# A diffusion step on one core: another share for the long convolution, a smaller prompt pool, and weight halves kept in DRAM

## The chip, the core and the metric

The kernel runs on one core of a Trainium2 chip. Its engines are TensorE (PE, matmuls; PEld loads its stationary operand), VectorE (DVE), ScalarE (ACT), GpSimd (POOL) and SyncE (SP). They run side by side, each through its own instruction queue in order, and wait for each other by semaphores; 16 DMA engines move data between DRAM and the core's memory (SBUF). The metric is the device time of one execution in microseconds, the median of several. Matmul results land in PSUM.

## What is computed

One trunk layer of a hybrid diffusion model, for 2048 latent tokens (`x_sample`) and 256 prompt tokens (`x_prompt`) of width 1024, all in float32. Cut to what matters here:

```python
def trunk_layer(x, cond, attend, ...):
    shift1, scale1, gate1, shift2, scale2, gate2 = adaln(cond, w_mod, b_mod)
    h = rms_norm(x, norm1_g) * (1.0 + scale1) + shift1
    u = h @ w_in                       # 1024 -> 256 pool + 768 hyena + 512 q + 512 k + 512 v
    y_pool = pool_mixer(u_pool, ...)   # centred windows 2/4/8/16
    y_hy = hyena_mixer(u_hy, ...)      # width-3 convolution, then two gated long convolutions by FFT
    q = rms_norm(u_q, q_norm_g); k = rms_norm(u_k, k_norm_g)
    y_na = attend(q, k, v)             # latent: 2-D neighbourhood and cached keys; prompt: dense
    x = x + gate1 * (concatenate([y_pool, y_hy, y_na]) @ w_out)
    h = rms_norm(x, norm2_g) * (1.0 + scale2) + shift2
    return x + gate2 * (square(relu(h @ w_up)) @ w_down), k, v
```

The same weights serve both groups of tokens. The outputs are both groups' tokens and the prompt's keys and values.

## The kernel before

**Precision.** A float32 matmul is done as three matmuls of a shorter type (float32r): `split` (L106) makes of each operand a high half (a copy that rounds, on ScalarE or POOL, L112 or L114) and a low half (operand less high half, L115), and `mm3` (L125) adds high by high, high by low and low by high. Weights come in tiles of 128 x 1024 (512 KB): `wtile` (L118) loads one by SP's queue into `wraw` (three buffers) and splits it into `wh` and `wl` (pool `w`, three buffers each); VectorE makes every low half.

**Streams.** The program is written as three generators that `weave` (L172) interleaves: `dense` (L1173), `latent_mixers` (L1050) and `prompt_mixers` (L851). Each yields a cost after each piece of work; `weave` always goes on with the stream whose sum of costs, divided by its share (2200e3, 850e3 and 700e3), is the least, and a stream that has to wait for another's result yields None until then, its sum standing still. This sets the order of the program and the priority of each instruction; the latent stream gets a lead of 1000 in priority and the prompt stream one of 2500. When the program is built, a list scheduler puts each engine's instructions into their final order by these priorities and by when their inputs and buffers are ready on its own timeline. I call the shares and this scheduler the planner.

**Dense.** The 2304 tokens are five runs: four of 512 latent tokens and one of 256 prompt tokens. First, in the order 0, 1, 2, 4 (the prompt), 3, each run is normalised and multiplied with the eight tiles of `w_u` (pool and convolution columns, L1193 to L1197), with 24 matmuls of the run's length on each tile. Then, in the order 3, 4, 0, 1, 2, `proj_qkv` (L257) multiplies each run with the twelve tiles of `w_qkv`, in six jobs of two tiles (L281, L282). The tokens are the stationary operand here and 256 columns of weights move, so that a job of a 512-token run is 96 matmuls; the first of its two tiles has its last use 12 matmuls before the end (L293, L294). The high half of the second tile of a job is made by POOL. After the projections the stream waits for the prompt stream (L1225), then runs `head` (output projection, L1084) and `mlp` (L1117) for the prompt and for the four latent runs.

**Latent mixers.** `filters` (L454) make the convolution's filters and bring them and the input to frequencies, with DFT matrices that POOL's queue loads (`dft_load`, L370). Then `hyena` (L615) does a spectral pass of 16 steps (`spectrum`, L622, in pool `p2v`), eight steps back to time and forth again (`inverse` and `fwd1`, pool `p2w`), a second spectral pass (pool `p2x`) and a last way back (`p2y`). Then comes the attention (L1065 on), which by the stream's order waits for the convolution, the projections and the prompt.

**Prompt mixers.** After the prompt's projections are written into the program (L852): the prompt's filters (L712), then in one pool `phy` the prompt's long convolution (L749) and the pooling of all tokens (L804), interleaved, then the prompt's attention (L922). The prompt's convolution begins with `conv3` (L563) for six channel tiles. Pools of SBUF are stacked from both sides: the prompt's lie on the right, beside those of the projections, and the latent mixers' on the left. A pool that covers an address of a closed pool waits for the last use of the tile that lay there.

Of the kernel before, what the change touches and what calls it, by code (L numbers as in the profile page):

```python
# [10 lines left out]
F32 = mybir.dt.float32  # L11
F32R = mybir.dt.float32r
# [7 lines left out]
P = 128  # L20
# [35 lines left out]
def tile_hybrid_step(ctx: ExitStack, tc: tile.TileContext, a: dict):  # L56
    nc = tc.nc
# [60 lines left out]
    def wtile(name, i, k, hi_eng=None):  # L118

        shape = [P, k, 1024 // k]  # L120
        raw = wp.tile(shape, F32, tag="wraw", name="wraw", bufs=3)
        nc.sync.dma_start(out=raw, in_=a[name][i].rearrange("p (k c) -> p k c", k=k))
        return split(wp, raw, shape, "w", nc.vector, hi_eng=hi_eng)

    def mm3(out, lh, ll, rh, rl, start, stop, **kw):  # L125
        nc.tensor.matmul(out, lh, rh, start=start, stop=False, **kw)  # L126
        nc.tensor.matmul(out, lh, rl, start=False, stop=False, **kw)  # L127
        nc.tensor.matmul(out, ll, rh, start=False, stop=stop, **kw)  # L128
# [28 lines left out]
    def normed(pool, x, r, g, s, k, bufs, keep=False):  # L157

        n = x.shape[1]
        t = xp.tile([P, 512], F32, tag="raw", name="xn", bufs=3)[:, :n] if keep else x  # L160
        if k % 2:
            hi = pool.tile([P, 512], F32R, tag="hh", name="hh", bufs=bufs)[:, :n]
            lo = pool.tile([P, 512], F32R, tag="hl", name="hl", bufs=bufs)[:, :n]
            nc.vector.scalar_tensor_tensor(out=t, in0=x, scalar=g, in1=r, op0=ALU.mult, op1=ALU.mult)  # L164
            nc.scalar.activation(hi, t, AF.Identity, bias=s)
            nc.vector.scalar_tensor_tensor(out=lo, in0=t, scalar=s, in1=hi.bitcast(F32), op0=ALU.add, op1=ALU.subtract)  # L166
            return hi, lo
        nc.gpsimd.tensor_tensor(out=t, in0=x, in1=r, op=ALU.mult)
        nc.vector.tensor_scalar(out=t, in0=t, scalar1=g, scalar2=s, op0=ALU.mult, op1=ALU.add)  # L169
        return split(pool, t, [P, 512], "h", nc.gpsimd, n=n, bufs=bufs)  # L170

    def weave(*streams):  # L172

# [83 lines left out]
    def proj_qkv(qp, hT, T0, n):  # L257

        todo = []

        def rows(dst, r0, cs):
            return dst[r0:r0 + 2 * P, cs].rearrange("(e p) c -> p e c", p=P)

        def finish(comp, part, t, raw, r, out):

            heads = raw.rearrange("p (e h d) -> p (e h) d", e=2, h=4)
            nc.vector.tensor_tensor(out=heads, in0=heads, in1=r[:, t // 32:t // 32 + 8, None].to_broadcast([P, 8, DH]), op=ALU.mult)
            tr = aux_tile()
            for c in range(2):
                for e in range(2):  # L270
                    nc.tensor.transpose(tr[:, (2 * c + e) * P:(2 * c + e + 1) * P], raw[:, e * 256 + c * P:e * 256 + (c + 1) * P], ident)
            nc.scalar.activation(out[:, :, t:t + 256], tr.rearrange("p (c t) -> p c t", c=2), AF.Copy, scale=(qg8, pvs("kg"))[comp])
            if t + 256 < n:
                return
            for c in range(2):
                j = 2 * part + c
                nc.sync.dma_start(out=(qT, kT)[comp][j][:, T0:T0 + n], in_=out[:, c])
                if comp == 1 and T0 == NL:
                    nc.sync.dma_start(out=a["new_kT"][j * P:(j + 1) * P, :], in_=out[:, c])

        for comp, part in JOBS:  # L281
            W = [wtile("w_qkv", 4 * comp + 2 * part + kk, 4, (None, nc.gpsimd)[kk]) for kk in range(2)]  # L282
            cs = slice(part * 256, (part + 1) * 256)
            out = raws = None
            if comp < 2:
                out = qp.tile([P, 2, 512], F32, tag="qo", name="qo")[:, :, :n]
                ss = qp.tile([P, 16], F32, tag="ss", name="ss")[:, :n // 32]
                raws = []
            for t in range(0, n, 2 * P):
                pp = acc_tile()  # L290
                for e in range(2):
                    ts = slice(t + e * P, t + (e + 1) * P)
                    for k in range(KD):  # L293
                        mm3(pp[:, e * 256:(e + 1) * 256], hT[k][0][:, ts], hT[k][1][:, ts], W[k // 4][0][:, k % 4, :], W[k // 4][1][:, k % 4, :], k == 0, k == KD - 1, skip_group_check=True)  # L294
                    if e == 0 and todo:
                        finish(*todo.pop(0))
                    yield 2600
                v = qp.tile([P, 512], F32, tag="q", name="v", bufs=3)
                nc.scalar.activation(v, pp, AF.Copy)
                if comp < 2:  # L300
                    sq = xp.tile([P, 512], F32, tag="tmp", name="sq")
                    nc.scalar.activation(sq, v, AF.Square)
                    nc.vector.tensor_reduce(out=ss[:, t // 32:t // 32 + 8], in_=sq.rearrange("p (h d) -> p h d", d=DH), axis=AX.X, op=ALU.add)
                    raws.append((t, v))
                    continue
                v2 = v.rearrange("p (e c) -> p e c", e=2)
                if T0 < NL:
                    nc.sync.dma_start(out=rows(vd, T0 + t, cs), in_=v2)
                else:
                    nc.sync.dma_start(out=rows(vpd, 0, cs), in_=v2)  # L310
                    nc.sync.dma_start(out=rows(a["new_v"], 0, cs), in_=v2)
            if comp < 2:
                r = rstd(qp, ss, DH, [P, n // 32], "small")
                todo += [(comp, part, t, v, r, out) for t, v in raws]
        while todo:
            finish(*todo.pop(0))
# [244 lines left out]
                fs1d.append((yield from filter_latent(o)))  # L561

    def conv3(hy, j, t0, L):  # L563
        u = hy.tile([P, L], F32, tag="cu", name="cu", bufs=2)
        nc.sync.dma_start(out=u, in_=uT[2 + j][:, t0:t0 + L])
        y = hy.tile([P, L], F32, tag="cy", name="cy", bufs=2)
        nc.scalar.activation(y, u, AF.Identity, scale=pvs("cw1", j), bias=pvs("cb", j))
        nc.vector.scalar_tensor_tensor(out=y[:, 1:L], in0=u[:, 0:L - 1], scalar=pvs("cw0", j), in1=y[:, 1:L], op0=ALU.mult, op1=ALU.add)
        nc.vector.scalar_tensor_tensor(out=y[:, 0:L - 1], in0=u[:, 1:L], scalar=pvs("cw2", j), in1=y[:, 0:L - 1], op0=ALU.mult, op1=ALU.add)
        return y  # L570
# [479 lines left out]
    def latent_mixers():  # L1050
        with scope("aps", 1, space=PSUM) as aps:
# [8 lines left out]
            yield from wait_for("u")  # L1060
            yield from wait_for("ln")
            with scope("hy") as kp:
                yield from hyena(kp, psum)
            done.add("hyena")
        yield from wait_for("qkv", "prompt")  # L1065
        with scope("att") as at, scope("attps", 2, space=PSUM) as aps:
# [106 lines left out]
    def dense(ms):  # L1173
# [3 lines left out]
        with scope("ln", side="right") as lp:  # L1177
# [8 lines left out]
            for i, b in enumerate(UORD):  # L1186
# [4 lines left out]
                if i < 4:  # L1191
                    xs = norm1_load(lp, *run_of(UORD[i + 1])[:2])
                for step, ct in enumerate((6, 2, 0, 7, 3, 4, 1, 5)):  # L1193
                    wh, wl = wtile("w_u", ct, 8)
                    pp = acc_tile()[:, :n]
                    for k in range(KD):
                        mm3(pp, wh[:, k, :], wl[:, k, :], hT[k][0], hT[k][1], k == 0, k == KD - 1)  # L1197
# [273 lines left out]
```

## Time and profile before

| | |
|---|---|
| median of 3 runs | 3198.05 us (3195.04 to 3200.3) |
| the profiled execution | 3199.58 us |
| its span, first to last instruction | 3197.7 us |
| TensorE (PE) busy | 3044.0 us, 95% of the span |
| its weight loads (PEld) | 2512.5 us, 79% |
| VectorE (DVE) busy | 1939.3 us, 61% |
| ScalarE (ACT) busy | 1427.5 us, 45% |
| GpSimd (POOL) busy | 958.1 us, 30% |
| mean granted clock of TensorE | 0.970 |
| moved by DMA | 494.26 MB, 154 GB/s of DRAM traffic over the span |

Times in the rows count from the first instruction. In a stage row, after each engine's busy time stands the number of its instructions (x); the granted clock is a share of full speed; the DMA share is the mean busy share of the 16 DMA engines. In a group row, `a<-b,c` names the output and inputs of an instruction, `x` its count, then busy time and mean duration, then the time that the engine sat idle just before, and what ended that. Matmuls overlap in TensorE, so their durations don't add up; what one takes in a dense stretch is the stretch's time by their count.

### The profile page before, as it was taken

How to read it: one execution, taken by the hardware profiler on the slowest of the kernel's cores; microseconds unless marked ns; L12 is line 12 of the kernel's file. 1: busy time of each engine (PE TensorE's matmuls, PEld its weight loads, DVE VectorE, ACT ScalarE, POOL GpSimd, SP SyncE). 2: the span in 40 equal slices, each digit the busy share in tenths (PEclk: the TensorE clock that was granted, in tenths of full speed). 3: DMA queues.
4: the chain of work that ended last, by engine and by line, in shares of the span. 5: the costliest groups of instructions: out<-in, count | busy, mean ns of one | idle time of the engine just before them, and what ended most of it. 6: DMA issues, size and time to landing. Idle time of an engine off the chain costs nothing.

```text
span 3197.7 us, 46181 instructions
## 1 busy us (share of the span) xinstructions
PE 3044.0 (95%) x16901; PEld 2512.5 (79%) x16901; DVE 1939.3 (61%) x3017; ACT 1427.5 (45%) x2721; POOL 958.1 (30%) x832
## 2 busy tenths in 40 slices
PE   5999999899898989999999999899999999999999
PEld 1667788799886879977887778688878888788887
DVE  7677676956777677878766545543564345644443
ACT  3555445545565566656555542332333223332222
POOL 2333233522543333446433321311231111311011
PEclk8999999999997899999999999899999999999999
DMA  6568667746973865553333335233324223332232
GB/s 223 161 211 296 218 208 235 250 149 215 291 240 113 273 194 176 181 183 101 121 118 109 104 110 176 79 93 102 115 92 145 95 97 113 98 119 99 92 99 86
DMA packets 255168, 494.26 MB, mean 155 GB/s; under 512 B 23763, under 2 KB 124824, under 8 KB 254619
## 3 DMA queue, kind: packets, MB, share of 16 engines
q1 hardware_dynamic: 247741, 469.03, 45.2%
q0 software_dynamic: 7200, 22.28, 2.5%
q8 instruction: 134, 2.20, 0.3%
q14 instruction: 93, 0.76, 0.1%
HBM read 421.86 MB, written 70.13 MB: 154 GB/s over the span
## 4 chain that ended last, share of the span: by engine, by line
PE 62%; DVE 2%; DMA 1%; ACT 1%; POOL 1%; issue 1%; SPq 0%; DVEq 0%; ACTq 0%; POOLq 0%
PE pm L126 18%; PE pm L128 18%; PE pm L127 18%; PE po L918 3%; PE ppt L897 2%; PE ps L883 1%; PE ps L884 1%; DVE xn L164 0%; DVE xn L169 0%; DVE wl L115 0%; DMA yraw<-yT 0%; DMA kin<-kT 0%; SPq L1009 0%; POOL ssq L150 0%; PE pm L154 0%
## 5 line engine op out<-in xcount | busy, mean ns | idle before, releaser
L115 DVE TENSOR_TENSOR wl<-wraw,wh 128x1024 fp32r<-128x1024 f32 x460 | 589.5, 1283 | 470.8 <-ACT wh L112 428.8
L112 ACT ACTIVATE wh<-wraw 128x1024 fp32r<-128x1024 f32 x430 | 454.6, 1058 | 781.1 <-PE pm L127 710.4
L126 PE MATMUL pm<-hh,wh 128*128 128x512 f32 (+1 forms) x1920 | 719.8, 377 | 19.6 <-ACT hh L112 11.4
L127 PE MATMUL pm<-hl,wh 128*128 128x512 f32 (+1 forms) x1920 | 718.2, 375 | 3.1 <-DVE hl L166 3.1
L128 PE MATMUL pm<-hh,wl 128*128 128x512 f32 (+1 forms) x1920 | 717.4, 374 | 0.0
L115 POOL TENSOR_TENSOR al<-r,ah 128x512 fp32r<-128x512 f32 (+1 forms) x160 | 199.5, 1248 | 967.0 <-ACT ah L112 966.8
L128 PE MATMUL pm<-ah,wl 128*128 128x512 f32 (+1 forms) x1280 | 475.7, 372 | 0.0
L127 PE MATMUL pm<-al,wh 128*128 128x512 f32 (+1 forms) x1280 | 473.3, 370 | 1.8 <-POOL al L115 1.8
L126 PE MATMUL pm<-ah,wh 128*128 128x512 f32 (+1 forms) x1280 | 473.2, 372 | 0.3 <-ACT wh L112 0.3
L126 PEld LDWEIGHTS pm<-hh,wh 128*128 128x128 f32 x1920 | 366.6, 191 | 101.0 <-issue 13.9
L127 PEld LDWEIGHTS pm<-hl,wh 128*128 128x128 f32 x1920 | 365.7, 190 | 74.5 <-issue 10.0
L128 PEld LDWEIGHTS pm<-hh,wl 128*128 128x128 f32 x1920 | 365.4, 190 | 70.0 <-issue 9.0
L1145 DVE SCALAR_TENSOR_TENSOR x<-pm,gate,x 128x512 f32<-128x512 f32 (+1 forms) x320 | 221.4, 695 | 274.1 <-PE pm L128 273.0
L127 PEld LDWEIGHTS pm<-al,wh 128*128 128x128 f32 x1280 | 240.9, 188 | 44.9 <-POOL al L115 2.0
L128 PEld LDWEIGHTS pm<-ah,wl 128*128 128x128 f32 x1280 | 240.9, 188 | 43.0 <-issue 1.7
L126 PEld LDWEIGHTS pm<-ah,wh 128*128 128x128 f32 x1280 | 240.6, 188 | 42.9 <-DVE x L1145 1.4
L127 PE MATMUL pm<-wl,hh 128*128 128x256 f32 x864 | 249.5, 291 | 5.3 <-DVE wl L115 5.3
L126 PE MATMUL pm<-wh,hh 128*128 128x256 f32 x864 | 247.6, 291 | 5.7 <-ACT hh L112 4.6
L128 PE MATMUL pm<-wh,hl 128*128 128x256 f32 x864 | 247.4, 291 | 3.9 <-POOL hl L115 3.1
L889 POOL TENSOR_SCALAR sS<-sS,rl 128x736 f32<-128x736 f32 (+5 forms) x128 | 126.7, 990 | 218.8 <-DVE rl L888 141.9
L127 PEld LDWEIGHTS pm<-wl,hh 128*128 128x128 f32 x864 | 167.2, 194 | 10.4 <-DVE wl L115 6.6
L126 PEld LDWEIGHTS pm<-wh,hh 128*128 128x128 f32 x864 | 166.5, 194 | 10.9 <-ACT hh L112 7.0
(325 smaller groups left out, 4841.1 us busy)
## 6 DMA issues: line engine op xcount, KB each, us to landing
wraw<-in_w_up SPq DMA_DIRECT2D x160, 512.0 KB
wraw<-in_w_down SPq DMA_DIRECT2D x160, 512.0 KB
wraw<-in_w_qkv SPq DMA_DIRECT2D x60, 512.0 KB
wraw<-in_w_u SPq DMA_DIRECT2D x40, 512.0 KB
dftw<-in_S POOLq DMA_DIRECT2D x40, 512.0 KB, 6.1
wraw<-in_w_out SPq DMA_DIRECT2D x40, 512.0 KB
x<-in_xT_sample SPq DMA_DIRECT2D x64, 256.0 KB
wm<-in_w_mod SPq DMA_DIRECT2D x64, 256.0 KB
```

The source lines that it names most:

```text
L112: nc.scalar.activation(hi, raw, AF.Copy)
L115: lo_eng.tensor_tensor(out=lo, in0=raw, in1=hi.bitcast(F32), op=ALU.subtract)
L126: nc.tensor.matmul(out, lh, rh, start=start, stop=False, **kw)
L127: nc.tensor.matmul(out, lh, rl, start=False, stop=False, **kw)
L128: nc.tensor.matmul(out, ll, rh, start=False, stop=stop, **kw)
L883: nc.tensor.matmul(out, qh[:, qc], krhs, start=True, stop=False, **kw)
L884: nc.tensor.matmul(out, ql[:, qc], krhs, start=False, stop=True, **kw)
L889: nc.gpsimd.tensor_scalar(out=sc_[:, :tot], in0=sc_[:, :tot], scalar1=r, scalar2=1.0, op0=ALU.mult, op1=ALU.mult)
L897: nc.tensor.transpose(tr[:n, q * P:(q + 1) * P], scs[e][:, so:so + n], ident)
L918: nc.tensor.matmul(po[64 * e:64 * e + 64, ocol:ocol + P], vap(e, n), pt[:n, col * P:(col + 1) * P], start=(q == 0), stop=(q == len(chunks) ...
L1145: nc.vector.scalar_tensor_tensor(out=xs[j], in0=po, scalar=gate2[:, j, c:c + 1], in1=xs[j], op0=ALU.mult, op1=ALU.add)
```

## The change

- `at_rate` (new) multiplies the costs that `hyena` yields by 0.55.
- `conv3`'s two tiles, in the prompt's pool `phy`, have one buffer each in place of two.
- `wtile_kept` (new) takes the place of `wtile` for `w_u` and `w_qkv`. In the first run of each (run 0 for `w_u`, run 3 for `w_qkv`) it loads and splits as before and also stores both halves in DRAM, by SP's queue. In the other four runs it loads the two halves by POOL's queue straight into `wh` and `wl`, and nothing is split. These are 20 split tiles with 40 stores, and 80 tiles with 160 loads, each of 512 KB.

```diff
+    halves_of = {"w_u": dtile([8, P, 2, 1024], "wud"), "w_qkv": dtile([12, P, 2, 1024], "wqd")}
+
+    def wtile_kept(name, i, k, first, hi_eng=None):
+        d = halves_of[name][i]
+        if first:
+            wh, wl = wtile(name, i, k, hi_eng)
+            for q, t in enumerate((wh, wl)):
+                nc.sync.dma_start(out=d[:, q].rearrange("p (k c) -> p k c", k=k), in_=t.bitcast(F32))
+            return wh, wl
+        shape = [P, k, 1024 // k]
+        hl = []
+        for q in range(2):
+            t = wp.tile(shape, F32R, tag="w" + "hl"[q], name="w" + "hl"[q])
+            nc.gpsimd.dma_start(out=t, in_=d[:, q].rearrange("p (k c) -> p k c", k=k))
+            hl.append(t)
+        return hl
...
+    def at_rate(stream, f):
+        for cost in stream:
+            yield cost and cost * f
...
-            W = [wtile("w_qkv", 4 * comp + 2 * part + kk, 4, (None, nc.gpsimd)[kk]) for kk in range(2)]
+            W = [wtile_kept("w_qkv", 4 * comp + 2 * part + kk, 4, T0 == 3 * 512, (None, nc.gpsimd)[kk]) for kk in range(2)]
...
-        u = hy.tile([P, L], F32, tag="cu", name="cu", bufs=2)
+        u = hy.tile([P, L], F32, tag="cu", name="cu", bufs=1)
...
-        y = hy.tile([P, L], F32, tag="cy", name="cy", bufs=2)
+        y = hy.tile([P, L], F32, tag="cy", name="cy", bufs=1)
...
-                yield from hyena(kp, psum)
+                yield from at_rate(hyena(kp, psum), 0.55)
...
-                    wh, wl = wtile("w_u", ct, 8)
+                    wh, wl = wtile_kept("w_u", ct, 8, i == 0)
```

## Rows read from the trace of the kernel before

**Rows 1.** Stages of the span; the first line names the columns.
```profile
core 0: us, PE busy (x) PEld busy (x) DVE busy (x) ACT busy (x) POOL busy (x), PEclk, DMA share, GB/s
68.00:394.00 326.00, 313.64 (x1433) 222.96 (x1433) 229.97 (x345) 168.31 (x299) 111.58 (x86) 0.97 0.68 218
394.00:596.00 202.00, 193.62 (x1369) 173.82 (x1369) 144.34 (x189) 100.01 (x194) 77.42 (x62) 0.98 0.73 244
596.00:942.00 346.00, 315.41 (x2382) 302.98 (x2383) 241.75 (x341) 174.17 (x345) 146.50 (x147) 0.96 0.68 217
942.00:1112.00 170.00, 143.84 (x909) 126.10 (x909) 126.45 (x187) 97.00 (x185) 60.88 (x58) 0.83 0.60 194
80.00:1112.00 1032.00, 957.25 (x6069) 819.20 (x6068) 730.70 (x1045) 531.06 (x1007) 388.57 (x347) 0.95 0.68 220
1112.00:1905.00 793.00, 771.52 (x5201) 644.01 (x5201) 549.42 (x1230) 461.68 (x1156) 322.60 (x305) 0.98 0.45 140
1905.00:3198.00 1293.00, 1270.12 (x5498) 1035.62 (x5496) 597.13 (x639) 403.77 (x514) 223.66 (x159) 0.99 0.33 108
```

**Rows 2.** Timeline of SP's DMA issues, 764 to 780 us: start, length, what.
```profile
766.91 0.38 SPq L662 DMA_DIRECT2D d1d<-sg  x1
767.40 0.42 SPq L122 DMA_DIRECT2D wraw<-in_w_qkv  x1
767.87 0.47 SPq L565 DMA_DIRECT2D cu<-uT  x1
...
769.56 1.15 SPq L810 DMA_DIRECT2D pw<-in_pool_w  x2
```

**Rows 3.** Single lines: count, ns min/median/max, first and last start (L747, L961, L1088).
```profile
L747 SPq DMA_DIRECT2D Fpd<-Fp x2: 326/367/408, 448.7 to 492.8; - x2
...
L961 SPq DMA_DIRECT2D yTp<-obp x4: 332/366/418, 953.0 to 1023.5; - x4
...
L1088 SPq DMA_DIRECT2D x<-in_xT_prompt x8: 333/420/437, 1023.9 to 1028.5; - x8
```

**Rows 4.** Stretches with one vector product of the spectral step alone (L649).
```profile
core 0: us, DVE busy (x), PEclk, DMA share, GB/s
526.00:645.00 119.00, 9.03 (x13) 0.91 0.76 248
645.00:767.00 122.00, 2.08 (x3) 1.00 0.47 148
767.00:895.00 128.00, 0.00 (x0) 0.96 0.91 300
895.00:1041.00 146.00, 11.11 (x16) 0.85 0.54 166
1041.00:1112.00 71.00, 0.00 (x0) 0.88 0.82 272
```

**Rows 5.** A slice of 80 us in the projections, columns as in Rows 1.
```profile
720.00:800.00 80.00, 77.04 (x641) 76.29 (x639) 50.66 (x71) 41.15 (x83) 22.96 (x24) 1.00 0.65 216
```

**Rows 6.** Groups by line and shape, 80 to 942 us: the weight splits.
```profile
L115 DVE TENSOR_TENSOR wl<-wraw,wh 128x1024 fp32r<-128x1024 f32 x99 | 135.4, 1372 | 64.2 <-POOL wh L114 30.8 <-ACT wh L112 29.4 <-POOL pE L818 1.9
...
L112 ACT ACTIVATE wh<-wraw 128x1024 fp32r<-128x1024 f32 x70 | 73.7, 1053 | 38.5 <-PE pm L127 34.0 <-DMA wraw<-in_w_out 2.9 <-issue 1.5
...
L114 POOL TENSOR_SCALAR wh<-wraw 128x1024 fp32r<-128x1024 f32 x30 | 35.0, 1166 | 148.4 <-PE pm L128 116.1 <-PE pm L127 23.8 <-issue 6.8
```

**Rows 7.** The DFT matrices' tile: POOL's issues (ns) and their landings (us).
```profile
L373 POOL DMA_DIRECT2D dftw<-in_S x40: 530/570/751, 202.2 to 1088.3; - x40
...
DMA to landing us min/median/max: 4.1/6.1/9.1
```

**Rows 8.** Waits of POOL, 80 to 942 us: total, times, longest.
```profile
POOL wh L114 <- PE pm L128: 116.1, 16, 11.6
```

**Rows 9.** Waits of PE, whole span: total, times, longest.
```profile
PE pm L127 <- DVE wl L115: 5.3, 4, 2.7
```

**Rows 10.** SP's loads of projection weights (L122), columns as in Rows 3.
```profile
L122 SPq DMA_DIRECT2D wraw<-in_w_qkv x60: 327/333/842, 358.8 to 890.9; - x60
```

**Rows 11.** Groups of PE by line, 942 to 1112 us: prompt's output projection and MLP.
```profile
L127 PE MATMUL pm<-hl,wh 128*128 128x256 f32 x125 | 35.5, 285 | 0.0
...
L127 PE MATMUL pm<-al,wh 128*128 128x256 f32 x32 | 8.9, 280 | 0.0
```

## Prediction

> **What bounds the kernel now.** I read the stages first: busy time of each engine, granted clock and DMA share in six stretches, cut where the trace shows the work to change [rows 1]. From 1112 us on TensorE is hardly ever idle and its clock is 0.98 to 0.99: attention and MLP are bound by TensorE, and whatever the change does before 1112 us is carried to the end one for one. The loss lies before. In 596 to 942 us TensorE is idle for 30.6 us, in 942 to 1112 us for 26.2 us, and there its granted clock is 0.83, a mean between the two levels of 1.2 and 2.4 GHz that comes with the gaps. Counting clock too, the stretch 942 to 1112 loses 26.2 + 0.17 x 143.8 = 51 us, and 596 to 942 loses 30.6 + 0.04 x 315.4 = 43 us.
>
> Second, why 942 to 1112 is empty. The dense stream (projections, then the prompt's output projection and MLP) may not go on before the prompt stream is through. The prompt's filters are stored by 493 us, but its attention stores its last output at 1023.5, and the loads of the prompt's output projection begin at 1023.9 [rows 3]. In between, the prompt's long convolution starts only at 767.9 [rows 2]. It isn't data that holds it: the pooling weights, an input that depends on nothing, start in the same microsecond, right behind the last store of the first spectral pass. So what was waited for is memory: the prompt's pool lies where the spectral pass had its tiles.
>
> Third, the latent convolution's pace [rows 4]. One of the vector products of a spectral step comes 13 times in 526 to 645 us (9.2 us a step), 3 times in the next 122 us, and 16 times in 895 to 1041 (9.1 us a step), although the dense stream has nothing to do for most of that. So a step has a chain of about 9.1 us, and 645 to 767 is a pause: there the order of the streams, not the chain, held the convolution back.
>
> **The change part by part.** The sum is made against the profiled execution: 3199.6 us, span 3197.7, 1.5 us over the median of 3198.05.
>
> *Share and pool.* The convolution's yields add up to 95.6 thousand units (two spectral passes of 31.2, 20.8 between them, 12.4 at the end); at 0.55 they count as 52.6. By the shares 850 and 2200 the planner spread them over 247 of the projections' 281 thousand units, and now over 136. The pause should go. With 9.1 us a step, 128 us for the middle part and 71 for the last [rows 4], a start at 526 gives 526 + 146 + 128 + 146 + 71 = 1017 us for the convolution's end, in place of about 1106. The prompt's pool gives up one of two buffers of 128 x 256 twice, 2 KB of a partition; its convolution can follow its filters at 493, and its attention the prompt's projection run. Single buffers make the six short convolutions of the prompt wait for each other; nothing on the path waits for them while the dense stream has two runs left. The end of the dense stream's wait then falls from 1024 to where the projections end, and TensorE has the prompt's projection and MLP to do beside the rest of the convolution. Of the 51 us of 942 to 1112 I take four fifths, **-40 us**, because the last passes keep their chain. Bounds: 0 (the hole only moves) and -94 (both stretches filled).
>
> *Splits removed.* Of 100 weight tiles of the projections, 80 are no longer split: 80 x 1.37 = 110 us of VectorE, 56 x 1.05 = 59 us of ScalarE and 24 x 1.17 = 28 us of POOL [rows 6]. These lie beside TensorE's work: it waited for a low half for 5.3 us in all [rows 9]. I take **-5 us**. 0 is one bound; the other is inside the -94 above, since a shorter VectorE queue can only close gaps.
>
> *Loads and stores of halves.* SP loses 80 issues (0.33 us each, 26 us [rows 10]) and gets 40 stores of 512 KB, 13 us by the same row; each store stands in SP's queue until the split is done, with the following loads behind it, in the first run of either projection only. A half is read back a run after its store, so that wait costs nothing: the other 7 or 11 tiles of the run lie between. POOL gets 160 loads. The nearest rows are those of the DFT matrices, which also come by POOL's queue in 512 KB: 0.57 us of POOL each and 6.1 us to landing, 4.1 to 9.1 [rows 7]. So POOL has 91 us more issue against the 28 saved, in a stretch where it is busy 389 of 1032 us [rows 1]: no bound by itself.
>
> The price is depth. Before, three raw tiles lay ahead of three split ones, and after a buffer came free a split of 1.05 + 1.37 us filled it. Now the load starts only when TensorE gives the buffer back. At 641 matmuls in 77 us (0.12 us each [rows 5]) a job of a 512-token run has 96 matmuls, 11.5 us, on two weight tiles. The first tile is given back 12 matmuls before the job ends, and the second tile of the next job, which takes its place, is wanted 12 matmuls after: 2.9 us. Two issues and a landing take 0.57 + 0.57 + 6.1 = 7.2 us. That is 4.3 us late in each of 24 jobs, 103 us, and for the prompt's run of the first projection (a tile each 2.9 us) 1.4 us on 8 tiles, 11 us. The dense stream waits; TensorE does so only where the other streams have no matmul ready. In 596 to 942 the projections' 1728 matmuls take 207 of 346 us, so two fifths of the time is other work or free, and the convolution and prompt attention of 942 to 1112 are added. I take five sixths of 114 us as covered: **+20 us**, bounds 0 and +114.
>
> On that landing time, "DMA: Bandwidth & Descriptors" of the Trainium skill (section "Anatomy of one DMA") fits 2.0 us plus bytes over 436e3 for a DMA of POOL's queue, 3.2 us for 512 KB. By it the halves would be 1.4 us late in a job, the term some 6 us and the time about 14 us lower; no row here lands so fast, since the fastest of 40 took 4.1 us [rows 7], so the trace is used.
>
> What stands behind the waiting triggers: POOL's queue is in order, and a trigger that waits for TensorE holds the splits of the spectral tiles and the hidden tiles behind it. It already did so for the split it shared in: 116.1 us in 16 waits [rows 8]. Twice as many such waits would be 116 us more on POOL. I take nothing, as the convolution has some 40 us of room before it is last; the upper bound is 24 x 7.3 us on its chain.
>
> *Bytes.* 120 more transfers of 512 KB, 62.9 MB. The 1032 us from 80 to 1112 moved 220 GB/s at share 0.68 [rows 1], 227 MB; with the new ones 290 MB. The busiest long stretch of the trace held 300 GB/s at 0.91 [rows 4]. At that rate 290 MB take 967 us: this work can't end before 1047, or 65 us earlier than now. That is the lower end of what I believe, and it says that the stage becomes crowded: loads of the spectral tiles will land later.
>
> Sum: -40 - 5 + 20 = -25 us: 3174.6 for a profiled execution, **3173** for the median.
>
> **Rivals.** *Slower: the halves come late and nothing covers them.* The place is the second weight tile of each projection job, and POOL's queue behind it. For it: a step of the convolution is a chain of some 9.1 us through every other engine, so it may have no matmul ready when one is wanted, and a stop of TensorE costs clock besides (0.83 after 942). Against it: in 596 to 942 two fifths of TensorE's time are not the projections. It decides from 45 us uncovered on, when under three fifths of the 114 us are filled. With a quarter filled: +86 - 45 = +41, about 3239.
>
> *No change: the hole moves.* The convolution's chain is as long as before, the queues are fuller by 62.9 MB, and each microsecond that the dense stream gains after 942 is lost between 394 and 942, where the same work is now done with later loads. For it: a share of 0.73 in 394 to 596 already, with 12.6 MB of stores and 6.3 MB of further loads put there. Time 3198, within 6 us.
>
> *The change does less than it says*: that the prompt's pool still meets the spectral tiles, or that the pause stays. It gives the terms 0 - 5 + 20, about 3213, and counts with the slower side.
>
> **How the numbers follow.** What a measurement of this kernel can tell is about 0.2%, 6.4 us. Forecast 0.50 (below 3191); late halves, with the case that the share does not pull, 0.37 (3205 to 3270); the hole moves 0.13. So faster 0.50, same 0.13, slower 0.37. Range 3125 to 3255: the low end is the bytes' bound and the splits (-65 - 5, with 3 for the rounding of the rates), the high end +57, half of the late halves uncovered with nothing gained; about 0.06 lies below it and 0.12 above. Both signs hold much of the chance; the forecast's own range is 3135 to 3191.
>
> **What would show it.** Right: the prompt's short convolution loads start before 560 us; no pause in the spectral steps, and the convolution's last store by 1040; the prompt's output projection begins within 20 us of the projections' end; TensorE's clock from 942 to 1112 over 0.93; the splits of the projections' weights 20 in number. Wrong: matmuls of the projections that wait for DMA landings of weight halves for over 45 us in total; spectral splits on POOL behind triggers that wait for TensorE; a clock under 0.95 between 500 and 900; a DMA share over 0.9 for hundreds of microseconds with the attention starting later than 1056. That is 1112 less the 56 us of matmuls that the prompt's output projection and MLP had done by then: 125 and 32 of each of three kinds [rows 11], at 0.12 us.

## The result and the profile after

The changed kernel takes 3237.91 us (median of 4 runs, 3233.68 to 3244.07) against 3196.55 for the kernel before beside it: a ratio of 1.0125, with a 95% interval of 1.0108 to 1.0143. It is 40 us slower where 25 us less was forecast. Below, a ratio is turned into microseconds by 1% = 32 us, and "after" is this kernel. Its lines are numbered some 20 higher from the new code on: the matmuls L126 to L128 are L145 to L147 now. The stores of halves stand in L134, their loads in L140.

First the stages, which answer to [rows 1], and one slice of 80 us. The columns are the same: in each stretch each engine's busy time with its count of instructions, then granted clock, DMA share and GB/s.

```profile
core 0: us, PE busy (x) PEld busy (x) DVE busy (x) ACT busy (x) POOL busy (x), PEclk, DMA share, GB/s
68.00:394.00 326.00, 306.64 (x1367) 212.90 (x1368) 181.15 (x296) 132.87 (x257) 133.96 (x147) 0.97 0.84 273
394.00:596.00 202.00, 182.52 (x1214) 164.78 (x1213) 124.38 (x181) 90.58 (x182) 74.76 (x79) 0.92 0.92 313
596.00:942.00 346.00, 299.00 (x2135) 271.71 (x2133) 200.17 (x321) 161.47 (x339) 160.74 (x193) 0.94 0.83 264
942.00:1112.00 170.00, 148.71 (x1150) 144.50 (x1151) 109.89 (x160) 89.57 (x166) 58.52 (x65) 0.93 0.70 226
560.00:640.00 80.00, 66.57 (x446) 56.05 (x446) 64.19 (x107) 44.79 (x100) 51.10 (x64) 0.94 1.02 334
```

The last of the four stages before 1112 has got better: 241 matmuls more than [rows 1] shows for it, and a clock of 0.93 for 0.83. The three before it have lost 66, 155 and 247 matmuls. VectorE and ScalarE are less busy than before in each of the four, so neither became the bound; what has grown is the DMA share, from 0.68, 0.73 and 0.68 to 0.84, 0.92 and 0.83.

Second, the marks of the order, which answer to [rows 2, 3]: the loads of the prompt's short convolutions, the stores of the prompt's attention, the loads ahead of the prompt's output projection and MLP, and the last stores of the latent convolution. Each row gives the count, the length in ns (least, median, most) and the first and last start.

```profile
L589 SPq DMA_DIRECT2D cu<-uT x6: 327/333/480, 537.3 to 590.6; - x6
L985 SPq DMA_DIRECT2D yTp<-obp x4: 320/395/975, 767.3 to 840.1; - x4
L1112 SPq DMA_DIRECT2D x<-in_xT_prompt x8: 328/328/647, 1049.5 to 1057.8; - x8
L734 SPq DMA_DIRECT2D yT<-yo x2: 320/332/343, 1111.9 to 1112.4; - x2
```

The prompt stream moved as meant: its short convolutions begin 230 us earlier, its attention is through 183 us earlier. Yet the dense stream comes to the prompt's output projection at 1049.5, where it was at 1023.9 [rows 3]: it no longer waits for the prompt, it is itself late. The last matmul of its projections starts at 1043, 105 us after that of the kernel before (938).

Third, the spectral steps, by one vector product alone as in [rows 4] (the same product, L673 now).

```profile
core 0: us, DVE busy (x), PEclk, DMA share, GB/s
572.00:716.00 144.00, 11.11 (x16) 0.92 0.78 253
744.00:893.00 149.00, 0.00 (x0) 0.99 0.89 283
893.00:1043.00 150.00, 11.11 (x16) 0.93 0.70 221
```

The long pause of [rows 4] is gone: the 16 products of the first pass stand between 572 and 716 us, some 9 us apart. The steps themselves have not become slower, but the middle part takes 149 us for 128.

### The profile page after: what moved, and what is told of

Same layout as the page of the kernel before. It is cut to its first block, busy times and chain, and to the rows that moved or that the text cites. A ratio compares the mean times of both kernels' runs of the same rounds, so it can differ in the third digit from the quotient of the medians.

```text
span 3231.8 us, 46139 instructions
## 1 busy us (share of the span) xinstructions
PE 3045.0 (94%) x16901; PEld 2507.8 (78%) x16901; DVE 1829.9 (57%) x2937; ACT 1380.6 (43%) x2665; POOL 982.8 (30%) x968
## 4 chain that ended last, share of the span: by engine, by line
PE 52%; DVE 2%; issue 0%; POOL 0%; ACT 0%; DVEq 0%; ACTq 0%; POOLq 0%
PE pm L145 16%; PE pm L147 16%; PE pm L146 16%; PE po L942 2%; PE ppt L921 1%; PE ps L907 1%; PE ps L908 1%; DVE xn L188 0%; DVE xn L183 0%; DVE wl L115 0%; DVE hl L185 0%; DVE m L1063 0%; DVE sS L1056 0%; PE pm L173 0%; POOL xn L187 0%
## 5 line engine op out<-in xcount | busy, mean ns | idle before, releaser
L145 PE MATMUL pm<-hh,wh 128*128 128x512 f32 (+1 forms) x1920 | 720.0, 377 | 20.6 <-ACT hh L112 11.4
L115 DVE TENSOR_TENSOR wl<-wraw,wh 128x1024 fp32r<-128x1024 f32 x380 | 481.6, 1268 | 440.6 <-ACT wh L112 421.4
L112 ACT ACTIVATE wh<-wraw 128x1024 fp32r<-128x1024 f32 x374 | 395.6, 1059 | 764.0 <-PE pm L146 718.7
L147 PE MATMUL pm<-hh,wl 128*128 128x512 f32 (+1 forms) x1920 | 718.0, 375 | 1.1 <-DMA wl<-wud 0.6
L145 PE MATMUL pm<-ah,wh 128*128 128x512 f32 (+1 forms) x1280 | 472.9, 372 | 10.0 <-DVE x L1169 10.0
L147 PE MATMUL pm<-ah,wl 128*128 128x512 f32 (+1 forms) x1280 | 477.4, 373 | 0.0
L145 PEld LDWEIGHTS pm<-hh,wh 128*128 128x128 f32 x1920 | 366.2, 191 | 103.5 <-issue 14.9
L147 PEld LDWEIGHTS pm<-hh,wl 128*128 128x128 f32 x1920 | 365.7, 190 | 73.1 <-issue 10.0
L145 PEld LDWEIGHTS pm<-ah,wh 128*128 128x128 f32 x1280 | 241.0, 189 | 53.2 <-DVE x L1169 11.7
L147 PEld LDWEIGHTS pm<-ah,wl 128*128 128x128 f32 x1280 | 241.9, 189 | 44.1 <-issue 2.5
L145 PE MATMUL pm<-wh,hh 128*128 128x256 f32 x864 | 253.8, 295 | 15.8 <-DMA wh<-wqd 8.1
L147 PE MATMUL pm<-wh,hl 128*128 128x256 f32 x864 | 249.0, 292 | 1.4 <-DVE hl L185 1.1
L145 PEld LDWEIGHTS pm<-wh,hh 128*128 128x128 f32 x864 | 170.0, 197 | 22.1 <-DMA wh<-wqd 10.3
L147 PEld LDWEIGHTS pm<-wh,hl 128*128 128x128 f32 x864 | 167.8, 196 | 7.3 <-issue 4.7
```

The costliest lines, as they stand in the source:

```text
L112: nc.scalar.activation(hi, raw, AF.Copy)
L115: lo_eng.tensor_tensor(out=lo, in0=raw, in1=hi.bitcast(F32), op=ALU.subtract)
```

## The experiments

Each kernel was timed in rounds against the kernel before on the same chip. The first ones split the change in parts.

**Order alone.** `w_u` and `w_qkv` are split in every run, as before; the share and the single buffers stay.

```diff
-            W = [wtile_kept("w_qkv", 4 * comp + 2 * part + kk, 4, T0 == 3 * 512, (None, nc.gpsimd)[kk]) for kk in range(2)]
+            W = [wtile("w_qkv", 4 * comp + 2 * part + kk, 4, (None, nc.gpsimd)[kk]) for kk in range(2)]
...
-                    wh, wl = wtile_kept("w_u", ct, 8, i == 0)
+                    wh, wl = wtile("w_u", ct, 8)
```

> The share of 0.55 and the single buffers of the prompt's pool alone; all 100 projection tiles are loaded and split as before. Theory A (the kept halves cost, the new order gains): faster than before by 20 to 45 us (3150 to 3177), projections' end under 1000 us, the first stage's end at 394 us as before. Theory B (the new order costs, because the convolution and the prompt now crowd the projections): slower by 20 to 40 us (3217 to 3237), with the convolution's end no earlier than 1100 us.

Measured: 3168.27 us, 0.9893 [0.9877, 0.9909], 34 us faster than before. Its stages and its marks:

```profile
68.00:394.00 326.00, 311.90 (x1437) 222.75 (x1438) 230.78 (x347) 169.40 (x301) 112.69 (x86) 0.98 0.68 219
394.00:596.00 202.00, 191.16 (x1288) 168.86 (x1287) 145.16 (x199) 99.72 (x203) 88.97 (x85) 0.96 0.73 242
596.00:942.00 346.00, 315.71 (x2342) 294.77 (x2342) 247.67 (x349) 179.63 (x362) 141.72 (x130) 0.95 0.66 215
942.00:1112.00 170.00, 156.65 (x1236) 153.15 (x1235) 135.66 (x187) 101.64 (x177) 64.53 (x66) 0.94 0.71 234
```

```profile
L589 SPq DMA_DIRECT2D cu<-uT x6: 320/519/1423, 522.5 to 567.3; - x6
...
L985 SPq DMA_DIRECT2D yTp<-obp x4: 320/356/413, 729.9 to 818.3; - x4
...
L1112 SPq DMA_DIRECT2D x<-in_xT_prompt x8: 328/424/1256, 985.1 to 992.5; - x8
L734 SPq DMA_DIRECT2D yT<-yo x2: 327/356/385, 1098.8 to 1099.3; - x2
```

The empty stretch of [rows 1] is filled (1236 matmuls for 909, clock 0.94 for 0.83). The convolution ends only some 7 us earlier than before (about 1106). What moved is the prompt, so that the dense stream goes on at 985, as soon as its projections end (977).

**Kept halves alone.** The diff's `at_rate` and both single buffers are taken back, `wtile_kept` stays.

> The kept halves alone, with the share of 1 and the double buffers of before. Theory A: slower by 30 to 60 us (3227 to 3257), the first stage's end at about 408 us as after the whole change, and the projections end later than 942 us. Theory B: within 10 us of before, or faster by VectorE's 110 us less work.

Measured: 3225.17 us, 1.0074 [1.0053, 1.0095], 24 us slower. The parts don't add: -34 and +24 make -10, and the whole change has +40. Put onto the new order, the halves cost 1.0125 - 0.9893 = 0.0232, 74 us; onto the old, 24 us. There the stretch with nothing to do took up much of what the projections lost: 942 to 1112 holds 1117 matmuls in that kernel, for 909 before.

**Kept `w_u` alone, kept `w_qkv` alone**, both with the new order. The edit of each is one half of the first diff above.

> The whole change, but the qkv tiles are loaded and split as before; only the eight tiles of the first projection are kept. Theory A: the cost of the halves splits by their stage: +14 us from the first projection, so the time is that of the new order alone plus 10 to 20 us. Theory B: as the new order alone, within 5 us.

> The whole change, but the tiles of the first projection are loaded and split as before; only the twelve qkv tiles are kept. Theory A: the new order alone plus 25 to 50 us, since here the loads of halves, the spectral steps and the prompt share POOL's queue and the DMA engines. Theory B: as the new order alone, within 5 us.

Measured: 3185.77 us, 0.9958 [0.9942, 0.9973] with `w_u` kept, and 3228.24 us, 1.0082 [1.0067, 1.0097] with `w_qkv` kept: 21 and 60 us over the order alone (for `w_u` 17 by the medians, the figure that a later expectation uses). So most of the cost comes with `w_qkv`, whose halves are loaded from 498 us on, where convolution and prompt run beside the projections, and less with `w_u`, loaded before 386 us.

**Single buffers alone**: the order alone, less the share.

```diff
-                yield from at_rate(hyena(kp, psum), 0.55)
+                yield from hyena(kp, psum)
```

> The single buffers of the prompt's pool alone: share 1, all tiles split as before. If the pool was what held the prompt until 767.9 us, the prompt's short convolution loads move to 500 to 560 us here too and most of the gain of the new order (33 us) is here: 3170 to 3180. If the share does the work, the prompt's start or the end of the convolution stays and the time is within 10 us of before.

Measured: 3196.04 us, 0.9998 [0.9986, 1.0011]. The time is that of before, but the trace isn't:

```profile
L589 SPq DMA_DIRECT2D cu<-uT x6: 319/398/584, 521.4 to 567.7; - x6
L1112 SPq DMA_DIRECT2D x<-in_xT_prompt x8: 328/420/597, 978.9 to 983.7; - x8
L734 SPq DMA_DIRECT2D yT<-yo x2: 327/342/357, 1163.6 to 1164.1; - x2
```

The single buffers alone let the prompt in at 521 and the dense stream on at 979. Then the convolution falls behind and ends at 1164 in place of 1106, and the attention behind it waits: the hole moves. The share brings that end back to 1099, and only then is there a gain. (The share with two buffers each was not run, so what the share does by itself isn't known.)

**Is it the bytes?** The order alone, with 120 transfers of 512 KB added that nothing waits for. First as copies from DRAM to DRAM, one with each weight load and two in the first runs:

```diff
...
+        if name in extra:
+            first = i not in seen.setdefault(name, set())
+            seen[name].add(i)
+            for _ in range(2 if first else 1):
+                j = next(extra[name])
+                nc.sync.dma_start(out=dump[j], in_=a[name][i])
```

> The new order with all tiles split as before (3168 us), plus 120 copies of 512 KB between places in DRAM that nothing waits for, one beside each later load and two beside each first one: the further transfers of the kept halves, without the halves. Theory bytes (the DMA engines are crowded, and spectral and weight loads land late): 40 to 70 us over the new order alone, 3208 to 3238. Theory queue (POOL's triggers hold its splits, and a load starts only when a buffer comes free): within 15 us of 3168.

Measured: 3284.46 us, 1.0284 [1.0269, 1.0299], but it answers another question. A copy with no input to wait for went out early:

```profile
L133 SPq DMA_DIRECT2D dump<-in_w_qkv x72: 488/488/587, 72.5 to 231.0; - x72
L133 SPq DMA_DIRECT2D dump<-in_w_u x48: 488/489/611, 21.3 to 139.5; - x48
```

All 120 lie in the first 231 us, and the first projection suffers there: 839 matmuls in 68 to 394, where the order alone has 1437. So the transfers were tied to their place: after each split the high half is stored (in the first run of each tile both halves), which makes 120 stores of 512 KB that nothing reads.

```diff
...
-        return split(wp, raw, shape, "w", nc.vector, hi_eng=hi_eng)
+        h, l = split(wp, raw, shape, "w", nc.vector, hi_eng=hi_eng)
+        if name in extra:
+            again = i in seen.setdefault(name, set())
+            seen[name].add(i)
+            for t in (h,) if again else (h, l):
+                nc.sync.dma_start(out=dump[next(slots)].rearrange("p (k c) -> p k c", k=k), in_=t.bitcast(F32))
+        return h, l
```

> The new order with all tiles split as before (3168 us), plus 120 stores of 512 KB: the high half of each later projection tile, both halves of each first one, right after its split, to places that nothing reads. These are the 62.9 MB of the kept halves, beside the same tiles, with raw tiles and splits as before. The copies between places in DRAM were all issued before 232 us and told nothing of this. Theory bytes: most of the 45 us that the halves cost when SP's queue loads them (3213), so 3200 to 3220. Theory depth (a load starts only when TensorE gives the buffer back): within 12 us of 3168.

Measured: 3200.19 us, 0.9993 [0.9981, 1.0005]. Nothing of the 34 us is left, though every split, load and wait of the order alone is still there. Its first three stages, and the largest wait of the stores in SP's queue (total, times, longest):

```profile
68.00:394.00 326.00, 315.49 (x1428) 223.17 (x1428) 229.35 (x341) 168.47 (x298) 106.75 (x85) 0.97 0.84 287
394.00:596.00 202.00, 185.00 (x1287) 165.93 (x1286) 136.15 (x184) 95.60 (x198) 79.54 (x73) 0.96 0.93 320
596.00:942.00 346.00, 301.61 (x2156) 274.97 (x2156) 231.87 (x333) 167.79 (x341) 136.14 (x133) 0.94 0.75 249
```

```profile
SPq L132 <- ACT wh L112: 64.2, 33, 6.9
```

These stores wait in SP's queue for the split, with the weight loads behind them, so bytes and queue both could be the cause. The same 120 stores with 8 KB each (`[:, 0:16]` of a tile on both sides) keep the instructions and much the same waits (the wait above is 74.0 us in 37 times there):

> As the run with 120 stores of 512 KB beside the splits (3200 us; by the ratios 32 us over the new order alone), but each store takes 16 of a row's 1024 columns, 8 KB in place of 512: the same instructions in SP's queue, the same waits for the splits, hardly any bytes. Theory bytes: the 32 us go, within 8 us of the new order alone by the ratios to the kernel before (0.987 to 0.992). Theory SP's queue (each store waits for a split with the loads behind it): it stays at 0.996 or more.

Measured: 3165.02 us, 0.9891 [0.986, 0.9923], as the order alone. The third stage has most of its matmuls back:

```profile
394.00:596.00 202.00, 192.08 (x1303) 169.16 (x1303) 149.36 (x199) 102.30 (x209) 89.17 (x88) 0.96 0.78 245
596.00:942.00 346.00, 313.24 (x2300) 293.48 (x2299) 248.67 (x350) 177.94 (x357) 142.05 (x128) 0.94 0.69 214
```

So 0.9993 - 0.9891 = 0.0102, 33 us (some 11 either way by the intervals), is the price of 62 MB of stores that nobody reads. A store also holds its split tile until it is through, but that isn't what costs here: the splits waited for a store 22.2 us in all, and 20.9 of these are one wait of POOL at its first split, where it waits in the order alone too (23.8 us, for TensorE).

**Is it POOL's queue?** The whole change, but SP's queue loads the halves.

```diff
-            nc.gpsimd.dma_start(out=t, in_=d[:, q].rearrange("p (k c) -> p k c", k=k))
+            nc.sync.dma_start(out=t.bitcast(F32), in_=d[:, q].rearrange("p (k c) -> p k c", k=k))
```

> The whole change, but SP's queue loads the halves in place of POOL's. The bytes and the depth stay; POOL gets no triggers. Theory bytes, and theory depth (the second tile of a job starts too late): within 15 us of the changed kernel's 3238. Theory POOL's queue (triggers that wait for TensorE hold the spectral splits behind them): 30 to 70 us less, 3168 to 3208.

Measured: 3213.53 us, 1.0065 [1.004, 1.0091]. By ratio that is 19 us less than after (some 10 either way by the intervals), so POOL's queue costs some 19 us. 23 us above the stores that nobody reads stay.

```profile
596.00:942.00 346.00, 295.29 (x2124) 270.38 (x2123) 198.57 (x314) 157.52 (x331) 124.02 (x120) 0.95 0.78 257
```

```profile
PE pm L145 <- DMA wh<-wqd: 12.5, 6, 4.0
```

The stage 596 to 942 is as poor as in after, with the direct waits for a half again small. What comes earlier is the convolution's last store, 1077 for 1112, and the end of the projections, 1019 for 1043. The same on `w_u` alone:

> Only the first projection's tiles are kept, and SP's queue loads their halves. With POOL's queue this took 17 us over the new order alone. Theory: those 17 us are POOL's triggers in front of its splits in the first stage, which ended at 394 us in the run with SP's loads; so 3160 to 3172 here. If the bytes did it: 3178 to 3190.

Measured: 3185.51 us, 0.9961 [0.9949, 0.9973], the same as through POOL's queue (0.9958). For the first projection the queue makes no difference to the time; its 19 us must come with `w_qkv` or with both together, which no run separates.

**Is it the depth?** SP's loads, and four buffers for each half in place of three. Room for these comes from one raw tile of three and one activation tile of nine, so a second kernel has that smaller room with three buffers.

```diff
+        bufs = 4 if tag == "w" else bufs
...
-        raw = wp.tile(shape, F32, tag="wraw", name="wraw", bufs=3)
+        raw = wp.tile(shape, F32, tag="wraw", name="wraw", bufs=2)
...
-            t = wp.tile(shape, F32R, tag="w" + "hl"[q], name="w" + "hl"[q])
-            nc.gpsimd.dma_start(out=t, in_=d[:, q].rearrange("p (k c) -> p k c", k=k))
+            t = wp.tile(shape, F32R, tag="w" + "hl"[q], name="w" + "hl"[q], bufs=4)
+            nc.sync.dma_start(out=t.bitcast(F32), in_=d[:, q].rearrange("p (k c) -> p k c", k=k))
...
-    hp = ctx.enter_context(tc.tile_pool(name="h", bufs=9))
+    hp = ctx.enter_context(tc.tile_pool(name="h", bufs=8))
```

> The whole change with SP's queue for the halves, and four buffers in place of three for each half of a weight tile; the room comes from one raw tile and one activation tile less, as in the run after this one. A job of the qkv projection uses two tiles, so four buffers let both tiles of the next job load during this one. Theory depth: 20 to 40 us under the run with the same room and three buffers. Theory bytes: within 8 us of it.

> The control for the four buffers: SP's queue for the halves, three buffers for each half, two raw tiles in place of three and eight activation tiles in place of nine. Theory: 3213 us plus what the smaller room costs the projections and the MLP, 0 to 20 us.

Measured: 3207.43 us, 1.0024 [1.0013, 1.0035] with four buffers, and 3209.19 us, 1.003 [1.0016, 1.0044] with three in the same room. The intervals overlap: a fourth buffer is worth 2 us by the ratios and 8 at most by the intervals, of the 74. It does act, though. The last matmul of the projections starts at 997 in place of 1023, but the last store of the convolution at 1120 in place of 1082, and the time stays. Both lie a little below the 1.0065 of SP's loads with the full room; why, no run shows, but a third raw tile isn't what the change lacked.

## Why the prediction was wrong

The direction was wrong, while the term of the new order was near its size. What failed are the terms of the kept halves. With -5 for the splits, +20 for late halves, and nothing for POOL's queue and for the bytes they make +15, and put onto the new order they measured +74. By the prediction's own steps:

**Share and pool: -40, measured -34.** Right in size, and in what it names as the reason, the prompt's place in memory. Wrong in one part: the convolution was to run without a pause and end at 1017. In the order alone it ends at 1099, and the pause is still there, 54 us without a product after 12 steps:

```profile
540.00:684.00 144.00, 8.34 (x12) 0.89 0.75 244
684.00:738.00 54.00, 0.00 (x0) 1.00 0.50 161
```

(The 9.1 us a step of [rows 4] is a little high: the stretches reach beyond their products, which stand 8 us apart from 911 to 1030. And the pooling weights of [rows 2] start 1.7 us after the convolution's load, not in the same microsecond. Neither changes the reading.) The gain comes from the prompt, out of the way at 819 us instead of 1024; the share only keeps the convolution from falling behind, as the single buffers alone show. "Clock over 0.93" in 942 to 1112 was met by the order alone (0.94), and in after just not (0.93).

**Splits removed: -5.** The splits went as counted. Of the 380 VectorE splits of weights that the page of after lists, 360 belong to other weights (160, 160 and 40 loads), so 20 are left.

```profile
L115 DVE TENSOR_TENSOR wl<-wraw,wh 128x1024 fp32r<-128x1024 f32 x380 | 481.6, 1268 | 440.6 <-ACT wh L112 421.4
...
wraw<-in_w_up SPq DMA_DIRECT2D x160, 512.0 KB
wraw<-in_w_down SPq DMA_DIRECT2D x160, 512.0 KB
...
wh<-wqd POOLq DMA_DIRECT2D x48, 512.0 KB, 7.6
...
wraw<-in_w_out SPq DMA_DIRECT2D x40, 512.0 KB
```

VectorE's 110 us less of work show nowhere in the time: it was not what TensorE waited for [rows 9], as the text said. No run takes the splits away without adding transfers, so the 5 us themselves are not measured.

**Late halves: +20, bounds 0 to +114.** The landings are slower than estimated: 7.6 us in the median for the high halves of `w_qkv` where 6.1 was taken. Yet TensorE hardly stands still for them. The waits for a half, by TensorE and by its weight loads, in the whole of 80 to 1112:

```profile
PE pm L145 <- DMA wh<-wqd: 8.1, 7, 2.3
```

```profile
PEld pm L145 <- DMA wh<-wqd: 10.3, 9, 2.5
```

That is under a fifth of the 103 us reckoned from 24 jobs, and well under the 45 us that the text had put up as the sign of this rival; four buffers gave nothing measurable either. By these waits the term was near its size. They count only the time in which TensorE stood still for a half, however: the dense stream did fall behind, by 66 us against the order alone (1043 for 977), and how much of that late halves are, no run separates.

**POOL's queue: nothing taken, some 19 us measured.** POOL's waits of 80 to 942, to set beside [rows 8]:

```profile
POOL wl L140 <- PE pm L147: 79.3, 26, 12.8
POOL wh L140 <- PE pm L147: 79.3, 19, 10.7
```

They make 159 us in 45 waits, against 116.1 in 16 and one more of 23.8 for the same split [rows 6], 140 in all. Half of the 159 belongs to `w_u`, where SP's queue gave no better time. So the waits grew by 19 us and not by 116, and that they, rather than the 160 starts of 0.54 to 0.57 us each, are what POOL's queue cost isn't shown. The step had counted on 40 us of room before the convolution is last; in after that end is at 1112, so there was none.

**Bytes: the step that failed most plainly.** The text counts 62.9 MB more and finds that at 300 GB/s the stages can't end before 1047. It used this only for the low end of the range, and gave the bytes no price of their own: "loads of the spectral tiles will land later" stands there without a number. That treats DMA as a limit that costs nothing until it is reached. The 62 MB of stores that nobody reads cost 33 us. In 596 to 942, at a mean share of 0.75, that kernel has 186 matmuls fewer than the order alone, (2342 - 2156) / 2342 = 8%. The share doesn't tell where the cost falls: in 394 to 596, at 0.93, the count is the same (1287 for 1288), and in 68 to 394, at 0.84, nearly so (1428 for 1437). The largest sum of any wait of TensorE in 394 to 1112 is 15.7 us, so no single wait in the trace carries the cost. All its waits there add up to 78 us for 53, and the growth is with the matmuls of the convolutions, the pooling and the prompt's attention (61 us for 32); those of the dense stream wait less (13 us for 20).

One place where it can be seen is the middle of the latent convolution, eight steps that load their inputs and DFT matrices from DRAM. These are the products of its way back to time, in the order alone, with the small stores, with the full stores and in after:

```profile
L702 DVE TENSOR_TENSOR z<-pf,xg x8: 680/692/692, 793.2 to 870.9; 128x512 f32<-128x512 f32 x8
L712 DVE TENSOR_TENSOR z<-pf,xg x8: 681/691/692, 787.6 to 863.7; 128x512 f32<-128x512 f32 x8
L712 DVE TENSOR_TENSOR z<-pf,xg x8: 665/691/692, 814.5 to 909.6; 128x512 f32<-128x512 f32 x8
L702 DVE TENSOR_TENSOR z<-pf,xg x8: 683/691/692, 753.7 to 868.5; 128x512 f32<-128x512 f32 x8
```

From first to last that is 78, 76, 95 and 115 us. The spectral steps don't show it: the first pass of the order alone took 12 us a step without any further bytes (12 products in 144 us, above), and that of after some 9.

**What the 74 us are.** Some 19 went with POOL's queue, 32 are what as many bytes cost as stores (0.9993 - 0.9893), and 23 stay open. This sum is argued, not shown. Two thirds of the halves' further bytes are loads and not stores, and the kernels lose their time in different places. The projections' last matmul in the order alone, with the stores, with SP's loads and in after:

```profile
L147 PE MATMUL pm<-wh,hl x864: 276/283/582, 393.8 to 977.0; 128*128 128x256 f32 x173
L157 PE MATMUL pm<-wh,hl x864: 274/283/583, 395.8 to 997.4; 128*128 128x256 f32 x173
L147 PE MATMUL pm<-wh,hl x864: 277/283/775, 392.3 to 1018.6; 128*128 128x256 f32 x173
L147 PE MATMUL pm<-wh,hl x864: 274/283/775, 408.5 to 1043.3; 128*128 128x256 f32 x173
```

The convolution's last store with the stores and with SP's loads (1099 in the order alone, 1112 in after):

```profile
L744 SPq DMA_DIRECT2D yT<-yo x2: 326/332/339, 1151.9 to 1152.4; - x2
L734 SPq DMA_DIRECT2D yT<-yo x2: 327/352/376, 1077.1 to 1077.5; - x2
```

With the stores it is the convolution that is late, by 53 us, and the projections by 20. With SP's loads the convolution ends 22 us before that of the order alone, and the projections end 42 us after. There the dense stream's matmuls wait 34 us in 394 to 1112, for 20 in the order alone, and 12.5 of these are for a half. So what stays open seems to lie with the dense stream, whose loads TensorE needs and whose buffers TensorE must free first. A fourth buffer or a third raw tile doesn't win it back. Loads of an eighth of the size with the same waits would tell bytes from waits there; that was not tried.

**The rivals.** The slower one gave the right time, 3239, and that is in part luck: its decisive term, weight tiles that come late uncovered, shows as 18 us of waits and not as 86, its second half, POOL's queue, is a quarter of the cost, and it gave the bytes no price either. It was right that the projections fall behind. The hole that moves was right about single buffers alone (3196), not about the change. Of the signs, the prompt's early convolution (537), its output projection close behind the projections, the spectral steps without a pause, the 20 splits and the low clock between 500 and 900 (0.94 in the row below) came true; the convolution's end by 1040 and the projections' waits over 45 us did not. The DMA share was over 0.9, at 0.92, for 202 us (394 to 596). The attention starts at 1144, but at 1130 in the kernel before, so that a start after 1056 could tell nothing.

```profile
500.00:900.00 400.00, 347.25 (x2459) 313.51 (x2458) 227.56 (x376) 188.34 (x405) 176.42 (x221) 0.94 0.86 277
```

The clock alone is a weak sign, though: the order alone has 0.94 in these 400 us too, and is 34 us faster than before.

**The better version.** The share and the single buffers without the kept halves take 3168.27 us and beat both kernels.

## What to carry to other kernels

To recompute was cheaper here than to keep in DRAM: before a change trades vector work for bytes, see whether the vector engine is what TensorE waits for (here 5 us [rows 9]), and give the bytes a price, not only a bound, where chains of transfers run beside the dense work; 62 MB of stores that nobody read cost 33 us here. Look for what a part of a change does to another: a hole in the schedule hides the cost of the kept halves (24 us), and filling it lays that cost open (74 us). And when a freed buffer lets one stream go early, ask at once which stream falls behind for it: with single buffers alone the hole moved from the prompt to the convolution, and the time stayed.

## What the runs showed of the hardware that was not expected

- Traffic had a price before the DMA engines were full, but not in proportion to their share. The order alone holds a share of 0.66 to 0.73 from 68 to 942. With the stores TensorE lost 8% of its matmuls in 596 to 942, at 0.75, and next to none in 68 to 394 and 394 to 596, at 0.84 and 0.93.
- The slice of 560 to 640 us in after moved 334 GB/s at a share of 1.02; the mean share of the profile can come out a little above 1. "DMA: Bandwidth & Descriptors" of the Trainium skill (section "Where 436 GB/s comes from") gives some 358 GB/s as a core's limit to its DRAM. The stages in which the stores cost 33 us had 249 to 320 GB/s. A slice of 80 us in the run with SP's loads (240 to 320 us) has 364 GB/s, so no trace here shows 358 as a bound.
- A DMA of 512 KB through POOL's queue landed in 5.1 us at the fastest and 7.6 in the median, 10.3 at most, in 394 to 1050 us of after (high halves):

```profile
DMA to landing us min/median/max: 5.1/7.6/10.3
```

  The 3.2 us of the fit that the prediction weighed ("Anatomy of one DMA" of the same page of the Trainium skill) came in none of these either.
- 120 more DMA instructions with their waits in SP's queue, of 8 KB each, cost nothing measurable (0.9891 and 0.9893, to within some 11 us), and the same with 512 KB cost 33 us.
- Which queue issues a load mattered by 19 us, with the bytes of both the same (557 MB). "DMA: Bandwidth & Descriptors" of the Trainium skill says under "Issuing engines are not separate DMA queues" that all DMAs run on the same 16 engines and that another issuer only saves the time to start them. The bytes' part agrees with it: SP's loads had the same crowded stages. The starts took POOL 0.54 to 0.57 us each, some 88 us for 160 of them, and it waited 159 us ahead of them; which of the two the 19 us come from, no run shows.
